# Relative-position bias written once and read back overlapping, and the order of the last matmul pair

## The chip, the cores and the metric

One core of one Trainium2 chip runs the whole kernel in one launch. The metric is the time of an execution on the device, in microseconds. Inputs and the output are float32 in device memory.

## The reference

The reference is a trunk of two layers over 256 tokens of 2048 features. Layer 0 is a differential attention with 8 heads, whose scores get a learned bias by relative position and a mask by chunks of 64 tokens, and a squared-ReLU MLP of width 8192. Then keys, values and forget gates are computed once, and layer 1 is a forgetting attention with 16 heads and a second MLP. RMS norms stand before each part and at the end. What the change touches is the bias of layer 0 (8 heads, 32 buckets):

```python
rel = key_pos[None, :] - q_pos[:, None]
bias = jnp.transpose(rel_table[t5_bucket(rel)], (2, 0, 1)).astype(f32)
mask = (key_pos[None, :] // CHUNK) <= (q_pos[:, None] // CHUNK)
s = jnp.where(mask, s + bias[None, :, None], NEG)
p = jax.nn.softmax(s, axis=-1)
```

and, in matmuls of every part, `h @ w_qkv`, `hn @ w_k`, `h @ w_q` and `h @ w_in`. The bias depends only on key position minus query position, so each head has one row of 383 values, of which a query sees 256 that shift by one from query to query.

## The kernel before, in words

Every product with a weight matrix is done in split precision. ScalarE rounds a raw weight tile to its high part (L180, tile whi), VectorE subtracts it from the raw tile to get the low part (L183, wlo), and the activations are kept as high and low parts side by side. TensorE adds the products of high with high, high with low and low with high.

The weights come in granules of 512 KB (128 x 1024 floats), 768 in all, loaded by SyncE's DMA queue (L172) into 4 raw buffers; high and low parts have 5 buffers each. A load goes out when the low part that used its raw buffer is done, so a granule is asked for about seven steps ahead of its use, and split about four steps ahead.

There are two kinds of units. Token-major units (mm_b, L194 to L196) are for values, output projections and the MLPs' second products: eight or more granules of 2 weight rows of 512 columns. Feature-major units (mm_a, L209 and L212) are for queries, keys and the MLPs' first products: four granules of 4 weight rows of 256 columns, each row in two halves of 128; each half takes one matmul of the high part with 512 columns (high and low activations) and one of the low part with 256 columns (high activations). In the last of the 16 rows (k == 15) the low part goes first, so that the matmul with the stop flag is the one that covers all 512 columns. After a unit, ScalarE copies the columns 256 to 511 of both halves (L315) and VectorE adds the columns 0 to 255 (L316).

The order of work is written out by hand. A list of steps has one granule each; at step s the lists pre[s], then the casts of later granules, mid[s], the low parts and loads, the matmuls of step s and post[s] are put out in this order, and each engine works through its own instructions in that order. A DMA takes its place in the instruction order of the engine that issues it, and the engine's later instructions wait behind a wait of it.

The bias is made at the start. At step 5 TensorE multiplies the table by a one-hot matrix (bias_rows, L338): 8 rows of 383 values. At step 6 VectorE copies them (L342), and SyncE writes them to F in device memory (L344), 128 times over for each head. At step 8 SyncE reads them back into T (L352): partition q gets, from copy q of each head, 256 values from an offset that moves back by one from copy to copy. POOL then masks 64 columns of the first 64 queries (L353). The softmax of each head uses T in VectorE's scaling of the scores (L415), first at about 86 us.

In step 6, ScalarE's squares for the first norm (L252) stand ahead of the bias in pre[6]; in step 8 the evacuation of the first value unit (L380) and the cast of the gate weights (L967) stand ahead of it in pre[8].

Of the kernel before, what the change touches and what calls it, by code (L numbers as in the profile page):

```python
# [11 lines left out]
F32 = mybir.dt.float32  # L12
# [8 lines left out]
P = 128  # L21
D = 2048
S = 256
HD = 128
FF = 8192
NA = 8
# [3 lines left out]
NEG = -1e30  # L30
# [4 lines left out]
NREL = 383  # L35
# [7 lines left out]
def kernel(ctx: ExitStack, tc: tile.TileContext, *args):  # L43
    (x, rel_table, attn_g, mlp_g, w_qkv, lq1, lk1, lq2, lk2, subln_g, w_o_a, kv_g,
     w_k, w_v, w_f, b_f, w_q, w_o_b, w_in, w_out, fin_g, onehot, out) = args
    nc = tc.nc
# [5 lines left out]
    dr = ctx.enter_context(tc.tile_pool(name="dr", bufs=1, space=DRAM))  # L52
# [29 lines left out]
    h = [sb.tile([P, 2, CW], F32, tag=f"h{c}", name=f"h{c}") for c in range(NCH)]  # L82
# [115 lines left out]
    def mm_a(u, g, k0):  # L198
        bank, xs = u.bank, u.xs()
        hi = g.hi.rearrange("p (k c) -> p k c", k=g.kk)  # L200
        lo = g.lo.rearrange("p (k c) -> p k c", k=g.kk)
        for j in range(g.kk):
            k = k0 + j
            xt = xs[k // 2][:, k % 2, :]
            for n in range(2):
                w = slice(n * P, (n + 1) * P)

                def whole():
                    nc.tensor.matmul(bank[n], hi[:, j, w], xt, start=k == 0, stop=k == 15)  # L209

                def part():
                    nc.tensor.matmul(bank[n][:, 0:S], lo[:, j, w], xt[:, 0:S], start=False, stop=False)  # L212

                if k == 15:
                    part()
                    whole()
                else:
                    whole()
                    part()


    def new_x(tag):
# [111 lines left out]
    bias = {}  # L334
# [5 lines left out]
    def bias_out():  # L340
        bs = sb.tile([NA, 512], F32, tag="e", bufs=2, name="bs")
        nc.vector.tensor_copy(out=bs[:, 0:NREL], in_=bias["p"][0:NA, 0:NREL])  # L342
        F = dr.tile([NA, P, NREL], F32, tag="F", name="F")
        nc.sync.dma_start(out=F, in_=bs[:, 0:NREL].unsqueeze(1).broadcast_to([NA, P, NREL]))  # L344
        bias["F"] = F

    def bias_in():
        T = sb.tile([P, NA, S], F32, tag="tnc", bufs=2, name="T")

        src = bias["F"].rearrange("h q r -> h (q r)")[:, 127:127 + P * (NREL - 1)]  # L350
        src = src.rearrange("h (q r) -> q h r", r=NREL - 1)[:, :, 0:S]
        nc.sync.dma_start(out=T, in_=src)  # L352
        nc.gpsimd.memset(T[0:64, :, 192:256], NEG)  # L353
        bias["T"] = T

    def build_lambda():
# [38 lines left out]
    def diff_head(hd):  # L395
# [13 lines left out]
        def softmax(qt):  # L409
            def run():  # L410
                nk = P * (qt + 1)
                sc = st["sc", qt]
                s = sb.tile([P, 2, S], F32, tag="ssb", bufs=2, name="ssb")
                b = bias["T"][:, hd, S - nk:S].unsqueeze(1).broadcast_to([P, 2, nk])
                nc.vector.scalar_tensor_tensor(out=s[:, :, 0:nk], in0=sc[:, :, 0:nk], scalar=SCALE, in1=b,  # L415
                                               op0=ALU.mult, op1=ALU.add)
                nm = sb.tile([P, 2], F32, tag="nm", bufs=2, name="nm")
                nc.vector.tensor_reduce(out=nm, in_=s[:, :, 0:nk], op=ALU.max, axis=AX.X, negate=True)
                e = sb.tile([P, 2, S], F32, tag="e", bufs=2, name="e")
                rs = sb.tile([P, 2], F32, tag="rsum", bufs=2, name="rsum")  # L420
                for c in range(2):
                    nc.scalar.activation(out=e[:, c, 0:nk], in_=s[:, c, 0:nk], func=AF.Exp,
                                         bias=nm[:, c:c + 1], accum_out=rs[:, c:c + 1])
                st["e", qt] = e, rs
            return run
# [497 lines left out]
    n, ng = len(order), len(grs)  # L923
# [27 lines left out]
    for k in range(2):  # L951
        w = slice(k * CW, (k + 1) * CW)
# [24 lines left out]
    n0.plan(7, lag=2)  # L977
    post[5].append(bias_rows)
    pre[6].append(bias_out)
    pre[8].append(bias_in)  # L980
    pre[12].append(build_lambda)

    ns = LA - 1
    for s in range(n + 2):
# [13 lines left out]
        if s < n:  # L998
            u, i, ms = order[s]
            if u.bank is None:  # L1000
                if u.apart:
                    u.bank = [ps.tile([P, 512], F32, tag="sc", name="sc") for _ in range(2)]
                else:
                    u.acc = ps.tile([P, 2, 512], F32, tag="acc", name="acc")
                    u.bank = [u.acc[:, m, :] for m in range(2)]
                if u.start is not None:
                    u.start(s)
            g = u.gs[i]
            if u.kind == "B":
                mm_b(u, g, 2 * i, ms)  # L1010
            else:
                mm_a(u, g, 4 * i)
            if i == len(u.gs) - 1:
                u.done(u, s, ms)
# [4 lines left out]

def bucket_onehot():  # L1020

    rel = np.arange(-255, NREL - 255)
    n = np.abs(rel)
    large = 8 + sum((n >= t).astype(np.int64) for t in (12, 16, 23, 32, 46, 64, 91))
    b = np.where(rel > 0, 16, 0) + np.where(n < 8, n, large)
    return (np.arange(32)[:, None] == b[None, :]).astype(np.float32)
# [25 lines left out]
```

## Time and profile before

| what | value |
|---|---|
| median of 3 runs | 2245.37 us (2244.74 to 2245.7) |
| the profiled execution's own time | 2244.49 us |
| its span, first to last instruction | 2242.7 us |
| mean granted TensorE clock | 0.994 |
| TensorE matmul busy | 2213.4 us |
| VectorE, ScalarE busy | 1356.7 us, 1020.8 us |
| moved by DMA | 416.06 MB, mean 186 GB/s |

An engine's busy time is the time in which its instructions run; starts are counted from the first instruction. Matmuls are pipelined, so that a row's duration is longer than the distance to the next start, and a stretch of TensorE is best read from the starts. The granted clock is a share of 2.4 GHz; 0.50 is 1.2 GHz. Issuing a DMA is not counted as busy time.

### The profile page before, as it was taken

What the parts mean: (1) busy time and instruction counts of PE and PEld (TensorE: products, weight loads), DVE (VectorE), ACT (ScalarE), POOL (GpSimd) and SP (SyncE); (2) the same over time, 40 slices, a digit from 0 to 9 for tenths busy, and PEclk for the clock granted to TensorE, in tenths of its full rate; (3) what the DMA queues carried; (4) which work ended last, traced back from release to release, by engine and by line L of the source; (5) the groups of instructions that cost most, each with busy time, mean ns of one, the idle gap of its engine ahead of it and who ended that gap; (6) DMA issues with size and microseconds to landing.
All of it is one profiled execution on the core that took longest, in us unless ns stands there. A gap on an engine that the chain in (4) does not pass through costs nothing.

```text
span 2242.7 us, 28986 instructions
## 1 busy us (share of the span) xinstructions
PE 2213.4 (99%) x11272; PEld 1877.7 (84%) x11272; DVE 1356.7 (60%) x1768; ACT 1020.8 (46%) x1343; POOL 13.6 (1%) x19
## 2 busy tenths in 40 slices
PE   8799999999999999999999999999999999999998
PEld 6688888888888888888888888888888888888886
DVE  4566666665565566566576566656655655655655
ACT  4455545544344344344554444454434444444443
POOL 0000000000000000000001000000000000000000
PEclk9899999999999999999999999999999999999999
DMA  7665555556656656655556565556566566566564
GB/s 199 199 183 172 166 170 183 173 188 201 183 185 202 195 180 195 192 187 189 177 170 204 173 194 186 180 170 201 183 200 189 185 193 186 188 197 180 187 202 135
DMA packets 319332, 416.06 MB, mean 186 GB/s; under 512 B 15066, under 2 KB 218972, under 8 KB 319068
## 3 DMA queue, kind: packets, MB, share of 16 engines
q1 hardware_dynamic: 319148, 414.20, 58.9%
q8 instruction: 88, 1.44, 0.3%
q14 instruction: 48, 0.39, 0.1%
q10 hardware_dynamic: 48, 0.02, 0.0%
HBM read 410.49 MB, written 3.68 MB: 185 GB/s over the span
## 4 chain that ended last, share of the span: by engine, by line
PE 97%; DMA 2%; DVE 0%; ACT 0%; issue 0%; SPq 0%; DVEq 0%; ACTq 0%
PE acc L209 32%; PE acc L212 16%; PE acc L194 15%; PE acc L196 15%; PE acc L195 15%; DMA raw<-in_w_qkv_a 2%; PE tp L232 1%; PE sc L405 0%; PE sc L748 0%; PE sc L194 0%; PE sc L195 0%; PE sc L196 0%; PE o L806 0%; DMA h<-in_x 0%; PE fp L619 0%; PE o L807 0%
## 5 line engine op out<-in xcount | busy, mean ns | idle before, releaser
L183 DVE TENSOR_TENSOR wlo<-raw,whi 128x1024 fp32r<-128x1024 f32 x767 | 926.1, 1225 | 627.4 <-ACT whi L180 626.8
L180 ACT CAST whi<-raw 128x1024 fp32r<-128x1024 f32 x767 | 795.9, 1048 | 730.5 <-PE acc L196 443.5
L209 PE MATMUL acc<-x,whi 128*128 128x512 f32 x2816 | 996.1, 399 | 17.5 <-ACT whi L180 17.5
L212 PE MATMUL acc<-x,wlo 128*128 128x256 f32 x2816 | 777.7, 281 | 0.5 <-DVE wlo L183 0.5
L209 PEld LDWEIGHTS acc<-x,whi 128*128 128x128 f32 x2816 | 525.7, 188 | 139.6 <-ACT whi L180 17.8
L212 PEld LDWEIGHTS acc<-x,wlo 128*128 128x128 f32 x2816 | 532.9, 189 | 9.2 <-DVE wlo L183 1.0
L194 PE MATMUL acc<-whi,hx 128*128 128x512 f32 x1120 | 436.9, 390 | 0.0
L196 PE MATMUL acc<-whi,hx 128*128 128x512 f32 x1120 | 436.0, 389 | 0.0
L195 PE MATMUL acc<-wlo,hx 128*128 128x512 f32 x1120 | 435.8, 389 | 0.0
L196 PEld LDWEIGHTS acc<-whi,hx 128*128 128x128 f32 x1120 | 210.2, 188 | 43.8
L195 PEld LDWEIGHTS acc<-wlo,hx 128*128 128x128 f32 x1120 | 210.3, 188 | 43.5
L194 PEld LDWEIGHTS acc<-whi,hx 128*128 128x128 f32 x1120 | 210.3, 188 | 43.1
L316 DVE TENSOR_TENSOR zs<-acc,z 128x512 f32<-128x512 f32 x96 | 66.3, 691 | 103.8 <-ACT z L315 103.8
L315 ACT COPY z<-acc 128x512 f32<-128x512 f32 x96 | 56.3, 587 | 157.9 <-PE acc L209 157.9
L590 ACT CAST hx<-s 128x512 fp32r<-128x512 f32 x64 | 39.7, 620 | 143.3 <-DVE s L588 143.3
L194 PE MATMUL acc<-whi,x 128*128 128x512 f32 x256 | 103.4, 404 | 0.0
L195 PE MATMUL acc<-wlo,x 128*128 128x512 f32 x256 | 100.5, 393 | 0.0
L196 PE MATMUL acc<-whi,x 128*128 128x512 f32 x256 | 100.5, 392 | 0.0
L209 PE MATMUL acc<-hx,whi 128*128 128x512 f32 x256 | 91.6, 398 | 0.0
L591 DVE TENSOR_TENSOR hx<-s,hx 128x512 fp32r<-128x512 f32 x64 | 44.3, 692 | 43.9 <-ACT hx L590 43.9
L212 PE MATMUL acc<-hx,wlo 128*128 128x256 f32 x256 | 70.5, 281 | 0.0
L327 DVE TENSOR_TENSOR h<-acc,h 128x512 f32<-128x512 f32 x88 | 56.7, 686 | 14.9 <-PE acc L196 14.9
(172 smaller groups left out, 1169.8 us busy)
## 6 DMA issues: line engine op xcount, KB each, us to landing
raw<-in_w_mlp_in SPq DMA_DIRECT2D x256, 512.0 KB, 4.0
raw<-in_w_mlp_out SPq DMA_DIRECT2D x256, 512.0 KB, 4.2
raw<-in_w_qkv_a SPq DMA_DIRECT2D x96, 512.0 KB, 4.5
raw<-in_w_o_a SPq DMA_DIRECT2D x32, 512.0 KB, 4.3
raw<-in_w_v_b SPq DMA_DIRECT2D x32, 512.0 KB, 3.8
raw<-in_w_k_b SPq DMA_DIRECT2D x32, 512.0 KB, 3.9
raw<-in_w_q_b SPq DMA_DIRECT2D x32, 512.0 KB, 4.2
raw<-in_w_o_b SPq DMA_DIRECT2D x32, 512.0 KB, 3.7
```

The source lines that it names most:

```text
L180: nc.scalar.copy(out=g.hi, in_=g.raw)
L183: nc.vector.tensor_tensor(out=g.lo, in0=g.raw, in1=g.hi, op=ALU.subtract)
L194: nc.tensor.matmul(bank[m], xh, hi[:, j, :], start=k == 0, stop=False)
L195: nc.tensor.matmul(bank[m], xh, lo[:, j, :], start=False, stop=False)
L196: nc.tensor.matmul(bank[m], xl, hi[:, j, :], start=False, stop=k == nk - 1)
L209: nc.tensor.matmul(bank[n], hi[:, j, w], xt, start=k == 0, stop=k == 15)
L212: nc.tensor.matmul(bank[n][:, 0:S], lo[:, j, w], xt[:, 0:S], start=False, stop=False)
L315: nc.scalar.copy(out=z1, in_=u.acc[:, :, S:2 * S])
L316: nc.vector.tensor_tensor(out=zs, in0=u.acc[:, :, 0:S], in1=z1, op=ALU.add)
L327: nc.vector.tensor_tensor(out=h[c][:, m, :], in0=u.bank[m], in1=h[c][:, m, :], op=ALU.add)
L590: nc.scalar.copy(out=t[:, :, 0:S], in_=s)
L591: nc.vector.tensor_tensor(out=t[:, :, S:2 * S], in0=s, in1=t[:, :, 0:S], op=ALU.subtract)
```

## The change: what it does

F now holds each head's 383 values once, in reversed order of position (the one-hot matrix is built with falling instead of rising positions). Both the write of F and the read of T are issued by ScalarE instead of SyncE, at the same places in the order. The read takes, for partition q and each head, the 256 values from offset q on, so that neighbouring partitions read overlapping pieces of the same row. T's columns are then in reversed order of keys; the mask is set on columns 0 to 63, and the softmax reads T backwards. In feature-major units all 16 rows put the high part first and the low part second, and the stop flag is on the low part's matmul.

```diff
@@ mm_a
             for n in range(2):
                 w = slice(n * P, (n + 1) * P)
-
-                def whole():
-                    nc.tensor.matmul(bank[n], hi[:, j, w], xt, start=k == 0, stop=k == 15)
-
-                def part():
-                    nc.tensor.matmul(bank[n][:, 0:S], lo[:, j, w], xt[:, 0:S], start=False, stop=False)
-
-                if k == 15:
-                    part()
-                    whole()
-                else:
-                    whole()
-                    part()
+                nc.tensor.matmul(bank[n], hi[:, j, w], xt, start=k == 0, stop=False)
+                nc.tensor.matmul(bank[n][:, 0:S], lo[:, j, w], xt[:, 0:S], start=False, stop=k == 15)
@@ bias_out, bias_in
-        F = dr.tile([NA, P, NREL], F32, tag="F", name="F")
-        nc.sync.dma_start(out=F, in_=bs[:, 0:NREL].unsqueeze(1).broadcast_to([NA, P, NREL]))
+        F = dr.tile([NA, NREL], F32, tag="F", name="F")
+        nc.scalar.dma_start(out=F, in_=bs[:, 0:NREL])
...
-        src = bias["F"].rearrange("h q r -> h (q r)")[:, 127:127 + P * (NREL - 1)]
-        src = src.rearrange("h (q r) -> q h r", r=NREL - 1)[:, :, 0:S]
-        nc.sync.dma_start(out=T, in_=src)
-        nc.gpsimd.memset(T[0:64, :, 192:256], NEG)
+        F = bias["F"]
+        src = bass.AP(F.tensor, F.offset, [[1, P], [NREL, NA], [1, S]])
+        nc.scalar.dma_start(out=T, in_=src)
+        nc.gpsimd.memset(T[0:64, :, 0:64], NEG)
@@ diff_head, softmax
-                b = bias["T"][:, hd, S - nk:S].unsqueeze(1).broadcast_to([P, 2, nk])
+                b = bias["T"][:, hd, 0:nk][:, ::-1].unsqueeze(1).broadcast_to([P, 2, nk])
@@ bucket_onehot
-    rel = np.arange(-255, NREL - 255)
+    rel = np.arange(127, 127 - NREL, -1)
```

## Rows read from the trace of the kernel before

**Rows 1.** The page, busy time (share of the span) and instructions of the engines.
```profile
PE 2213.4 (99%) x11272; PEld 1877.7 (84%) x11272; DVE 1356.7 (60%) x1768; ACT 1020.8 (46%) x1343; POOL 13.6 (1%) x19
```
**Rows 2.** Stretches: from:to, length, engines' busy time (instructions), granted clock, DMA share, GB/s.
```profile
40.00:60.00 20.00, 9.41 (x56) 8.00 (x54) 2.36 (x2) 1.01 (x2) 0.00 (x0) 0.79 0.56 77
60.00:80.00 20.00, 12.62 (x58) 10.53 (x59) 9.28 (x13) 7.79 (x10) 0.52 (x1) 0.70 0.74 224
...
300.00:1000.00 700.00, 700.00 (x3547) 594.26 (x3547) 421.49 (x494) 308.76 (x370) 0.00 (x0) 1.00 0.60 187
```
**Rows 3.** Waits of TensorE from 20 to 75 us: total, times, longest.
```profile
PE acc L209 <- ACT whi L180: 17.5, 1, 17.5
PE acc L212 <- DVE wlo L183: 0.5, 1, 0.5
```
**Rows 4.** Chain of waits, 20 to 75 us: start, us, what.
```profile
35.57 30.16 DMA raw<-in_w_qkv_a
```
**Rows 5.** Timeline of SyncE's queue: start, duration, DMA issued (several merged).
```profile
29.44 0.82 SPq L344 DMA_DIRECT2D F<-bs  x1
35.57 13.97 SPq L172 DMA_DIRECT2D raw<-in_w_qkv_a  x2
64.38 0.37 SPq L352 DMA_DIRECT2D T<-F  x1
64.85 5.13 SPq L172 DMA_DIRECT2D raw<-in_w_qkv_a  x4
```
**Rows 6.** Waits of SyncE's queue from 20 to 75 us.
```profile
SPq L352 <- DMA F<-bs: 14.8, 1, 14.8
```
**Rows 7.** Stretches of 4 us, columns as in rows 2.
```profile
32.00:36.00 4.00, 4.00 (x20) 3.07 (x19) 1.61 (x5) 3.20 (x6) 0.00 (x0) 1.00 1.00 329
...
56.00:60.00 4.00, 0.00 (x0) 0.00 (x0) 0.00 (x0) 0.00 (x0) 0.00 (x0) 0.50 0.46 49
...
68.00:72.00 4.00, 3.83 (x12) 3.35 (x13) 1.58 (x3) 0.92 (x2) 0.52 (x1) 0.50 1.09 378
```
**Rows 8.** Timeline of TensorE's matmuls; L209 is the high part, L212 the low.
```profile
49.13 0.28 PE L212 MATMUL acc<-x,wlo 128*128 128x256 f32 x1
66.91 0.80 PE L209 MATMUL acc<-x,whi 128*128 128x512 f32 x1 [17.50 <-ACT whi L180]
...
72.29 0.39 PE L209 MATMUL acc<-x,whi 128*128 128x512 f32 x1
...
77.23 0.40 PE L209 MATMUL acc<-x,whi 128*128 128x512 f32 x1
...
78.64 0.40 PE L209 MATMUL acc<-x,whi 128*128 128x512 f32 x1
```
**Rows 9.** Timeline of ScalarE: the casts of granules (two merged in a row).
```profile
33.25 1.98 ACT L180 CAST whi<-raw 128x1024 fp32r<-128x1024 f32 x2
...
39.01 2.00 ACT L180 CAST whi<-raw 128x1024 fp32r<-128x1024 f32 x2
...
71.37 1.05 ACT L180 CAST whi<-raw 128x1024 fp32r<-128x1024 f32 x1 [3.08 <-DMA raw<-in_w_qkv_a]
```
**Rows 10.** Timeline of VectorE: the bias copy and low parts.
```profile
28.87 0.55 DVE L342 COPY bs<-bp 8x383 f32<-8x383 f32 x1 [0.17 <-PE bp L338]
...
34.32 1.23 DVE L183 TENSOR_TENSOR wlo<-raw,whi 128x1024 fp32r<-128x1024 f32 x1 [4.91 <-ACT whi L180]
...
40.10 2.36 DVE L183 TENSOR_TENSOR wlo<-raw,whi 128x1024 fp32r<-128x1024 f32 x2 [0.25 <-ACT whi L180]
```
**Rows 11.** DMAs: one issue's duration; KB and us to landing; weight loads' landing, 24 to 75.
```profile
0.98 0.38 ACTq L94 DMA_DIRECT2D grow<-in_attn_norm_g  x1
...
grow<-in_attn_norm_g ACTq DMA_DIRECT2D x1, 16.0 KB, 2.7
...
C<-fg_nc SPq DMA_DIRECT2D x1, 16.0 KB, 4.7
...
NC<-C SPq DMA_DIRECT2D x4, 512.0 KB, 6.1
...
DMA to landing us min/median/max: 4.7/6.5/30.2
```
**Rows 12.** Who uses T: the mask on POOL, and the softmax's instructions (ns).
```profile
69.84 0.52 POOL L353 MEMSET T<- 64x512 f32 x1 [67.33 <-DMA T<-F]
...
L415 DVE SCALAR_TENSOR_TENSOR ssb<-sc,T x16: 415/554/685, 86.2 to 334.8; 128x256 f32<-128x256 f32 x8, 128x512 f32<-128x512 f32 x8
```

## The prediction

> **What bounds the kernel now.** I read the page's busy times first: TensorE works 99% of the span [rows 1], so only what stops or slows TensorE can matter. The stretch view says where the missing per cent lies: TensorE is busy 9.41 us of the 20 us from 40, at a granted clock of 0.79, and 12.62 us of the next 20 at 0.70, while the 700 us from 300 are full at 1.00 [rows 2]. The list of waits names the stop: one wait of 17.5 us of a high-part matmul for ScalarE's cast L180, and 0.5 us for the low part [rows 3]. The chain of waits goes one step further back: the cast waited for a weight load issued at 35.57 that took 30.16 us to land [rows 4].
>
> Why so long is read from SyncE's queue. At 29.44 it issued the write of F (8 x 128 x 383 x 4 bytes = 1.57 MB, out of 8 partitions). The two loads issued behind it, at 35.57 and after, held the queue 13.97 us in the issuing alone; then the read of T waited 14.8 us for F and went out at 64.38 [rows 5, 6]. In between the DMA engines were busy to 0.46 and moved 49 GB/s, against 329 GB/s before and 378 GB/s after [rows 7]. So F crawls on about half of the engines for 34.9 us (29.44 to 64.38), and the loads behind it in the same queue crawl with it. The stop is a DMA queue's, shown on TensorE.
>
> **What the stop costs.** Call a 512-column high matmul and its 256-column low one a pair. From 72.29 to 77.23 there are 14 pairs, 0.353 us each [rows 8]. The last low matmul before the stop starts at 49.13 and is followed a third of a pair later, so the next high one was due at 49.25; it starts at 66.91, and the engine is back at full speed only with the one at 72.29. Seven pairs run between 66.91 and 72.29, which cost 7 x 0.353 = 2.47 us at full clock. Lost: (66.91 - 49.25) + (5.38 - 2.47) = 17.66 + 2.91 = 20.57 us; the second term is the 0.5 us wait and the half clock (1.2 instead of 2.4 GHz) that the idle stretch left behind.
>
> **The change part by part.**
>
> F becomes 8 rows of 1532 bytes, 12 KB, and goes to ScalarE's queue. The bulk write is gone, and with it what the loads of granules 13 and 14 queued behind: -20.57 us if nothing else is late at that place. The steps are numbered as TensorE takes granules of 8 pairs, 2.82 us: granule 13 is the one due at 49.25, so 11 is due at 43.6, 14 at 52.1, 15 at 54.9, 16 at 57.7.
>
> ScalarE now issues two DMAs in its instruction order. F stands behind the eight squares of step 6, that is at 33.25 instead of 29.44; its source was copied by VectorE at 28.9 [rows 10], so it waits for nothing. The one DMA that this queue issued before cost 0.38 us, F's old issue on SyncE 0.82 [rows 5, 11]; I take 0.4. Behind it stand the casts of granules 9 and 10 (33.25 -> 33.65) and, through them, the low parts, the load of granule 13 (35.57 -> 36.0) and the norm chain. T's issue stands at step 8 behind the value evacuation and the cast of the gate weights; the casts of granules 11 and 12, at 39.01 before [rows 9], come behind it: 39.01 + 0.4 + 0.4 = 39.8. VectorE's low parts of 11 and 12 then end at 42.1 and 43.3 instead of 41.3 and 42.5 (1.23 each [rows 10]); 11 is due at 43.6, so 1.5 us are left, and both issues cost TensorE nothing. Without that cover they would cost 0.8 us.
>
> T's issue waits on ScalarE for F's landing. Transfers of 16 KB landed in 2.7 us at the start on ScalarE's queue and in 4.7 us later on SyncE's [rows 11], so F lands at 36.4 to 38.4, before ScalarE reaches T at 39.4: no wait. Bounds: 0, and 3.5 us under the first rival.
>
> One rule speaks against this. The Trainium skill (DMA: Bandwidth & Descriptors, "Queues, rings and completion order") states that a transfer's completion signal lands only after every earlier write of the same DMA engine, across its queues. By it F's landing would also wait for the four weight loads issued up to 29.1; no row here shows such a wait. Taken with the median of 6.5 us to landing of the loads of this stretch [rows 11] it would come at about 35.6, still ahead of 39.4, so by the rule the sum stays, and the first rival gets a part of its chance from it.
>
> T's megabyte now runs beside the weight loads in another queue. The nearest row: T and the two loads behind it, issued from 64.38 on, were in by 71.37, 7.0 us, at 378 GB/s [rows 5, 7, 9]. Used for granules 14 and 15, loaded at 39.6 and 42.1: in by 46.6 and 49.1, cast a microsecond later, due at 52.1 and 54.9. Granule 13, loaded at 36.0, lands by 43.0 even if it takes as long as that. Cover of 3 us or more everywhere: 0. The other end is F's own rate of 49 GB/s, which is the second rival. T itself is wanted by the softmax at 86.2 [rows 12], 20.57 earlier now, at 65.6; it is in by about 47 and its mask takes POOL 0.52 us.
>
> The mask on columns 0 to 63 and the one-hot table's order cost nothing. The reversed read of T on VectorE: 16 instructions of 0.415 to 0.685 us [rows 12], 8.8 us in all. No row shows a backward operand; between no change and twice the time I take no change. Even 8.8 us more would be spread over 250 us of an engine that is 60% busy, beside a TensorE that is not waiting for it: 0.
>
> The matmul order. 96 feature-major units (16 + 64 + 16) end today with low, high, low, high on their last row, which puts two short matmuls together and, at the next unit's start, two long ones. From the high matmul at 77.23 to the one at 78.64 lies such a place, 1.41 us for four pairs; four regular ones cost 4 x 0.353 = 1.41 [rows 8]. So the order is worth 0; by the rounding of the starts (0.02 us a place) between -1.9 and +1.9 us. The evacuation's first copy reads only columns that the last short matmul no longer writes, and may start 0.12 us sooner; TensorE does not wait for it.
>
> **Sum.** The profiled execution took 2244.49 us: 2244.49 - 20.57 = 2223.92. The median of the runs shown is 0.88 above it: 2224.8.
>
> **Rivals.**
>
> *ScalarE is held at T's issue*, by F's landing or because the issuing itself blocks, as SyncE's did behind F. If it is held until T is in (5.5 us, as from 64.38 to the mask at 69.84 [rows 5, 12]), granule 11 is cast at 44.9 to 46.0 and its low part ends at 47.2 against 43.7: 3.5 us, 2228.3. For it: the blocked issues of SyncE. Against it: those had F's 1024 pieces ahead of them, ScalarE's queue has 8; T's issue took 0.37 us once F was done.
>
> *T's read is the new crawl*: 128 partitions read overlapping pieces of the same 12 KB, beside the loads. At 49 GB/s T takes 21.4 us, to 61.2, and if granule 14 is held as long, TensorE stops from 52.1 to 62.2 and has 2.9 us of half clock: 13.1 us given back, 2237.9. It turns the change into a loss when T takes over 29.3 us (in at 68.7): 16.6 + 1.05 + 2.9 = 20.6 us of new stop. For it: no row shows this overlapping read. Against it: a broadcast read of 512 KB out of few rows landed in 6.1 us [rows 11], and the half-idle engines went with a transfer out of 8 partitions, T goes to 128.
>
> *The stop is not F's*: loads would be late there anyway, 2245.4. For it: what TensorE waited for was a weight load. Against it: loads landed within 1.5 us of F's end, and at 329 GB/s before F had the engines.
>
> **How the numbers follow.** Forecast 84% (2222.8 to 2226.8 by the order's bounds); ScalarE held 8%; T's crawl 3% short of a loss and 2% as a loss; not F's 3%. The range takes in the forecast's bounds and the first rival: 2222.8 to 2229. A measurement of this kernel can tell about 0.2%, 4.5 us, from no change: faster 0.95, no change 0.03, slower 0.02.
>
> **What would show it.** Right: no wait of L209 for L180 after 40 us; granted clock 1.00 from 40 to 80; F landing in under 5 us, T in under 10, both on ScalarE's queue; some 1.5 MB and 1000 packets less in all; softmax operations of unchanged length; the high matmul that stood at 72.29 at about 51.7. Wrong: a TensorE wait near 43.6 (ScalarE held) or near 52 (T), or a pair count in which a unit's end costs more than 1.41 us.

## The result, and the profile after

The changed kernel takes 2226.38 us (median of 4 runs, 2225.32 to 2227.27) against 2245.19 (4 runs); the ratio is 0.9916, with a 95% interval of 0.9899 to 0.9933. The forecast was 2224.8.

The page's busy times and its DMA total of the kernel after; the total was 416.06 MB in 319332 packets before.

```profile
span 2224.6 us, 28985 instructions
...
PE 2211.4 (99%) x11272; PEld 1875.3 (84%) x11272; DVE 1357.0 (61%) x1768; ACT 1020.6 (46%) x1343; POOL 13.3 (1%) x19
...
DMA packets 318317, 414.50 MB, mean 186 GB/s; under 512 B 15067, under 2 KB 217957, under 8 KB 318053
```

Stretches of the kernel after, columns as in [rows 2]:

```profile
40.00:60.00 20.00, 20.00 (x117) 17.43 (x116) 14.45 (x21) 10.62 (x14) 0.52 (x1) 1.00 0.87 261
60.00:80.00 20.00, 20.00 (x118) 17.47 (x117) 14.46 (x23) 9.74 (x17) 0.00 (x0) 1.00 0.64 203
```

TensorE is full and at its upper clock where it stood [rows 2]. From 20 to 75 us the list of its waits is empty; the waits of [rows 3] are gone.

ScalarE and its queue in the kernel after (timeline; ACTq is the issuing of a DMA):

```profile
33.77 0.63 ACT L241 ACTIVATE junk<-h 128x512 f32<-128x512 f32 x1
33.84 0.51 ACTq L333 DMA_DIRECT2D F<-bs  x1
34.31 0.19 ACT L241 ACTIVATION_READ_ACCUMULATOR junk<-h 128x1 f32 x1
34.40 1.99 ACT L180 CAST whi<-raw 128x1024 fp32r<-128x1024 f32 x2
38.71 0.69 ACT L369 ACTIVATE v<-acc,rstd 128x512 f32<-128x512 f32 x1 [2.32 <-DVE rstd L261]
39.12 0.40 ACTq L341 DMA_DIRECT2D T<-F  x1
39.30 0.68 ACT L369 ACTIVATE v<-acc,rstd 128x512 f32<-128x512 f32 x1
39.87 0.41 ACT L956 CAST wfs<-wf_raw 128x256 fp32r<-128x256 f32 x1
40.16 2.95 ACT L180 CAST whi<-raw 128x1024 fp32r<-128x1024 f32 x3
47.05 1.05 ACT L180 CAST whi<-raw 128x1024 fp32r<-128x1024 f32 x1 [3.93 <-DMA raw<-in_w_qkv_a]
```

Both DMAs are issued while ScalarE still computes what stands ahead of them: F at 33.84 beside the last square, T at 39.12 beside the value evacuation. The casts behind them stand 1.15 us later than in [rows 9], and this profile as a whole is 1.12 us late by then (below). T goes out without waiting for F. It landed 6.4 us after its issue and was masked at 45.59 (69.84 before); the softmax instructions that read it backwards keep their lengths, 415, 554 and 685 ns.

Where the time went is read best by pairing the matmuls of the two runs: 11272 in each, in the same order but for the last rows of units. Three starts serve as marks: the first feature-major matmul, the one at 72.29 in [rows 8], and the last one of all. Timeline of TensorE, first the kernel before, then after:

```profile
34.62 0.50 PE L209 MATMUL acc<-x,whi 128*128 128x512 f32 x1
...
2233.09 0.39 PE L196 MATMUL sc<-whi,hx 128*128 128x512 f32 x1
```

```profile
35.74 0.50 PE L207 MATMUL acc<-x,whi 128*128 128x512 f32 x1
...
50.43 0.40 PE L207 MATMUL acc<-x,whi 128*128 128x512 f32 x1
...
52.90 0.40 PE L207 MATMUL acc<-x,whi 128*128 128x512 f32 x1
...
2215.01 0.39 PE L196 MATMUL sc<-whi,hx 128*128 128x512 f32 x1
```

| | to the first mark | first to second | second to last |
|---|---|---|---|
| before | 34.62 | 37.67 | 2160.80 |
| after | 35.74 | 17.16 | 2162.11 |
| difference | +1.12 | -20.51 | +1.31 |

The matmul of 66.91 stands at 50.43, and the seven pairs behind it take 2.47 us. So the stop gave back 20.51 us; 1.12 were lost ahead of it and 1.31 behind it.

### The profile page after: what moved, and what is told of

Same layout as the page of the kernel before. It is cut to its first block, busy times and chain, and to the rows that moved or that the text cites. A ratio compares the mean times of both kernels' runs of the same rounds, so it can differ in the third digit from the quotient of the medians.

```text
span 2224.6 us, 28985 instructions
## 1 busy us (share of the span) xinstructions
PE 2211.4 (99%) x11272; PEld 1875.3 (84%) x11272; DVE 1357.0 (61%) x1768; ACT 1020.6 (46%) x1343; POOL 13.3 (1%) x19
## 4 chain that ended last, share of the span: by engine, by line
PE 99%; DMA 0%; DVE 0%; ACT 0%; SPq 0%; issue 0%; DVEq 0%; ACTq 0%
PE acc L207 32%; PE acc L208 16%; PE acc L194 15%; PE acc L196 15%; PE acc L195 15%; PE tp L221 1%; PE sc L737 0%; PE sc L394 0%; PE sc L196 0%; PE sc L194 0%; PE sc L195 0%; PE o L795 0%; DMA h<-in_x 0%; PE fp L608 0%; PE o L796 0%; PE tpo L472 0%
## 5 line engine op out<-in xcount | busy, mean ns | idle before, releaser
L207 PE MATMUL acc<-x,whi 128*128 128x512 f32 x2816 | 998.9, 399 | 0.0
L208 PE MATMUL acc<-x,wlo 128*128 128x256 f32 x2816 | 790.6, 281 | 0.0
L207 PEld LDWEIGHTS acc<-x,whi 128*128 128x128 f32 x2816 | 529.1, 188 | 130.0
L208 PEld LDWEIGHTS acc<-x,wlo 128*128 128x128 f32 x2816 | 532.0, 189 | 0.9
L207 PE MATMUL acc<-hx,whi 128*128 128x512 f32 x256 | 91.9, 401 | 0.0
L208 PE MATMUL acc<-hx,wlo 128*128 128x256 f32 x256 | 71.9, 281 | 0.0
L316 DVE TENSOR_TENSOR h<-acc,h 128x512 f32<-128x512 f32 x88 | 56.6, 685 | 14.9 <-PE acc L196 14.9
```

The lines of the kernel that those rows point to most:

```text
L316: nc.vector.tensor_tensor(out=h[c][:, m, :], in0=u.bank[m], in1=h[c][:, m, :], op=ALU.add)
```

## The experiments

The same three differences, read in the same way from each run's trace:

| run | what | median us | ratio to before (95%) | start | to second mark | rest |
|---|---|---|---|---|---|---|
| changed kernel | | 2226.38 | 0.9916 (0.9899 to 0.9933) | +1.12 | -20.51 | +1.31 |
| e9 | the same again | 2225.41 | 0.9912 (0.9897 to 0.9927) | 0.00 | -20.52 | +1.31 |
| e1 | bias part alone | 2223.82 | 0.9906 (0.9892 to 0.9919) | +0.01 | -20.62 | -0.11 |
| e2 | order part alone | 2246.44 | 1.0006 (0.9997 to 1.0014) | +0.02 | +0.35 | +1.73 |
| e3 | bias part, SyncE's queue | 2225.27 | 0.9913 (0.9899 to 0.9926) | -0.13 | -20.52 | +1.31 |

**e1, bias part alone, and e2, order part alone.** Edits: the `mm_a` hunk taken back, and the `mm_a` hunk alone.

> The bias part of the change alone (the matmul order of before). Theory: the whole gain is the removed write of F. Then the stop at granule 13 is gone and the time is that of before less 20.5 us, 2224.7, less what the order part costs in the changed kernel: aligned matmul by matmul, the changed kernel gains 20.5 us at the stop, loses 1.1 us ahead of it and 1.3 us spread over the rest. If the 1.3 us are the order's, this run is 1.3 us faster than the changed kernel (about 2225); if they are chance, the two agree. Rival (the order part carries some of the gain): slower than the changed kernel by more than 2 us.

> The order part alone (F written in bulk and read back as before). Theory: the stop stays, and the order costs 0.5 to 1.5 us: 2245.7 to 2246.7, with the pairs of some attention units at 353 ns instead of 347. Rival (order is worth something): below 2243.

Measured: 2223.82 and 2246.44. Without the order part the stop's 20.6 us come back and nothing is lost afterwards; with it the rest is longer by 1.3 us beside the bias part and 1.7 alone (0.5 of these right behind the second mark). So the gain is the bias part's alone, and the order part costs something. By the intervals of the ratios that cost cannot be told from none; it is the paired starts that show it.

**e9, the changed kernel again.**

> The changed kernel once more, unedited, beside the next two. Its first profile began 1.1 us later than the kernel before, at TensorE's wait for the first load of x; in five other profiles of kernels with the same start this difference was between -0.2 and +2.1 us. Theory (a chance of the first load's landing): another start here, within -0.3 and +2.2 us, the rest as before, -20.5 at the stop and +1.2 to +1.4 after it; 2224.5 to 2227.5. Rival (the change makes the start slower): again 1.1 us.

Measured: 2225.41; no late start, the other two differences as before. The 1.12 us at the start were a chance of that profile: TensorE waited 2.5 us for the first load of x there, 0.5 us in the kernel before, 0.7 in e9 and between 0.7 and 2.2 us in other runs.

**e3, both DMAs on SyncE.**

```diff
-        nc.scalar.dma_start(out=F, in_=bs[:, 0:NREL])
+        nc.sync.dma_start(out=F, in_=bs[:, 0:NREL])
...
-        nc.scalar.dma_start(out=T, in_=src)
+        nc.sync.dma_start(out=T, in_=src)
```

> F written once and T read overlapping as in the changed kernel, but both issued by SyncE instead of ScalarE. Theory (the bytes and pieces of F were the cost, not whose queue it was): no stop, within 1 us of the changed kernel, 2225 to 2227.5; F goes out 4 us earlier, T's read stands ahead of two loads in one queue. Rival (the move to another queue is what freed the loads): TensorE waits near 43 to 55 us, 2230 or more.

Measured: 2225.27, no TensorE wait. The move to ScalarE's queue is worth nothing: with F small, T's read went out of SyncE's queue at 39.56 without a wait and the loads behind it were in time.

**e4, F written late.** F's write moved from step 6 to step 8, right ahead of T's read.

```diff
-    pre[6].append(bias_out)
+    pre[8].append(bias_out)
     pre[8].append(bias_in)
```

> F's write issued by ScalarE at step 8, right ahead of T's read, instead of step 6, so that ScalarE stands at T's issue for F's whole landing. Theory (cover of 1.5 us for the low part and 2.7 us for the high part of granule 11, F lands 2.5 to 4 us after its issue): the casts of granules 11 and 12 come 2.5 to 4.5 us later and TensorE stops 1 to 3 us near 43.6: 2227.5 to 2229.5. Rival (more cover than counted, or ScalarE does not stand): same as the changed kernel, under 2227.

Measured: 2227.42 (0.9921, 0.9906 to 0.9936). Waits from 20 to 75 us of ScalarE, then of TensorE (whole run), then ScalarE's queue:

```profile
ACT whi L180 <- DMA F<-bs: 4.1, 1, 4.1
```

```profile
PE acc L208 <- DVE wlo L183: 0.8, 1, 0.8
PE acc L207 <- ACT whi L180: 0.5, 1, 0.5
```

```profile
41.13 0.51 ACTq L333 DMA_DIRECT2D F<-bs  x1
43.59 0.40 ACTq L341 DMA_DIRECT2D T<-F  x1
44.02 3.89 ACT L180 CAST whi<-raw 128x1024 fp32r<-128x1024 f32 x4 [4.10 <-DMA F<-bs]
```

T can go out 2.5 us after F's issue began. The casts waited 4.1 us, and TensorE lost 1.8 us at granule 11 (its stretch between the first two marks is 18.98 us against 17.16). That is the first rival's mechanism, at the place it named, made to happen by a later F; the cover at that place is about 2 us. The time is 0.1 us below the range that was expected.

**e5, e6, e7, e12: what made the old write expensive.** Each is the changed kernel plus a write of the old F's bytes that nobody reads, so that no instruction waits for it.

```diff
+        G8 = dr.tile([NA, P, NREL], F32, tag="G8", name="G8")
+        nc.sync.dma_start(out=G8, in_=h[0][0:NA, 0, 0:NREL].unsqueeze(1).broadcast_to([NA, P, NREL]))
```

That is e5, behind F's write at step 6 (the profile calls the new tile G). In e6 it is issued by `nc.scalar` behind T's read; in e7 its source is `h[0][:, 0, 0:NREL]`, 128 partitions with 8 copies each; in e12 a piece has 384 floats.

> The changed kernel, and beside it a write of the old F's size and shape (1.57 MB, 1024 pieces of 1532 bytes out of 8 partitions, from a tile of x, which nobody reads) issued by SyncE at step 6, where F's write stood. No instruction waits for it. Theory (loads queue behind such a write): the stop at granule 13 is back, 17 to 18 us plus some 3 us of half clock, 2243 to 2247. Rival (what cost the time was that T waited for F and held SyncE's queue): no such wait here, so no stop of that size, under 2232.

> The changed kernel with the same extra write issued by ScalarE right behind T's read, in ScalarE's queue, which carries nothing else later; again nobody waits for it. Theory A (only the order within one queue hurts; across queues the DMA engines take turns and a load passes the slow write): at most small stops, 2226 to 2231. Theory B (a slow piece holds its engine for about 0.27 us whoever comes next: 34.9 us for 128 pieces per engine): loads alternate with slow pieces on the 8 engines and land in 9 to 10 us or more, TensorE is starved for part of some 33 us: 2233 to 2245.

> The changed kernel with an extra write of the same 1.57 MB in the same 1024 pieces of 1532 bytes, but out of 128 partitions, issued by SyncE at step 6. Theory (8 source partitions, not the bytes, make the write slow): it runs on all 16 engines at 300 GB/s or more, 4 to 5 us, and the loads behind it are 4 to 5 us late, which the cover of some 4 to 6 us takes: no stop or under 2 us, 2226 to 2229. Rival (1.57 MB of writes is slow from anywhere): stop of over 10 us, 2237 or more.

> As the run with the extra write in SyncE's queue (1024 pieces of 1532 bytes out of 8 partitions, 2247 us, stop back), with pieces of 1536 bytes, 384 instead of 383 floats. Theory (few source partitions make the pieces slow): the stop is back all the same, 2244 to 2249. Rival (the odd length of 1532 bytes makes them slow; the packet records show 214 to 228 ns a piece of it out of 8 partitions against 84 ns for 2048-byte pieces of the loads): pieces at some 70 ns, the write done in about 10 us, stop under 3 us, 2226 to 2230.

| run | extra write | median us | ratio to before (95%) |
|---|---|---|---|
| e5 | 8 partitions, SyncE's queue | 2247.38 | 1.001 (1.0 to 1.0019) |
| e12 | the same, 1536-byte pieces | 2247.52 | 1.0011 (1.0001 to 1.002) |
| e6 | 8 partitions, ScalarE's queue | 2242.33 | 0.9987 (0.9978 to 0.9997) |
| e7 | 128 partitions, SyncE's queue | 2227.05 | 0.9919 (0.9903 to 0.9936) |

TensorE's waits from 20 us on in e5, in e6 and in e7 (L207 is the high part, L208 the low):

```profile
PE acc L207 <- ACT whi L180: 15.4, 2, 10.1
PE acc L208 <- DVE wlo L183: 0.9, 2, 0.5
```

```profile
PE acc L207 <- ACT whi L180: 8.8, 2, 6.1
PE acc L208 <- DVE wlo L183: 1.4, 3, 0.5
PE sc L396 <- DVE k L311: 1.1, 1, 1.1
```

```profile
PE acc L208 <- DVE wlo L183: 1.4, 2, 0.8
PE acc L207 <- ACT whi L180: 0.3, 1, 0.3
```

A write that nobody waits for brings the whole stop back (e5). TensorE waits twice there, and ScalarE's timeline tells for what:

```profile
33.43 0.51 ACTq L333 DMA_DIRECT2D F<-bs  x1
...
48.30 0.40 ACTq L343 DMA_DIRECT2D T<-F  x1
48.74 1.99 ACT L180 CAST whi<-raw 128x1024 fp32r<-128x1024 f32 x2 [8.88 <-DMA F<-bs]
68.05 1.04 ACT L180 CAST whi<-raw 128x1024 fp32r<-128x1024 f32 x1 [17.32 <-DMA raw<-in_w_qkv_a]
```

The longer wait, 10.1 us, stands at granule 13, as the stop of the kernel before does: its load, issued behind the extra write, was in only at 68.05. That alone sets when TensorE goes on, at 69.14. The first wait, 5.3 us at granule 11, is the first rival's: F's 12 KB, in ScalarE's queue and beside the write, let T go out 14.9 us after F's issue (2.5 in e4), and the casts behind T waited 8.9 us. It takes up part of a stop that the load would have made in any case. So T's wait on SyncE's queue is not needed for the stop; in the kernel before, too, the load that TensorE waited for was issued at 35.57, ahead of T's read in that queue [rows 5].

In ScalarE's queue the write costs 5 us less than in e5, but goes out 8.3 us later, at 38.22 behind T's read (e6). There the DMA view gives the loads' median landing in that stretch, 38 to 80 us:

```profile
raw<-in_w_qkv_a SPq DMA_DIRECT2D x10, 512.0 KB, 16.3
G<-h ACTq DMA_DIRECT2D x1, 1532.0 KB
T<-F ACTq DMA_DIRECT2D x1, 1024.0 KB, 7.2
```

16.3 us instead of the 5.3 that the changed kernel has from 28 to 66 us. Two loads land at 60.4 and 68.7, ahead of the write's last piece at 72.5: loads get past the slow write, and still starve. The Trainium skill (DMA: Bandwidth & Descriptors, "Queues, rings and completion order") states that an engine goes round the queues it has work for; these landings agree with it. The same bytes and pieces out of 128 partitions cost 2.3 us by the paired starts (e7); by the packet records they moved in 8.8 us, against 30.2 in e5. (That is half as fast as e7's expectation had it; the times of e6, by its theory B, of e7 and of e12 lie inside their ranges, that of e5 0.4 us above.) The trace's packet records give the piece: a median of 214 ns for a 1532-byte piece out of 8 partitions in e5, 228 in the kernel before, 74 out of 128 partitions in e7. Rounding the piece to 1536 bytes changes nothing (e12, 213 ns). Why a piece is three times slower there is open: the number of source partitions, the engines in use and the layout of the target went together.

**e8, e10, e11: the matmul order.** The order's cost led to three other orders of a feature-major row: high, low, low, high (e8); eight high then eight low of a granule (e10); high, high, low, low (e11).

```diff
-            for n in range(2):
-                w = slice(n * P, (n + 1) * P)
-                nc.tensor.matmul(bank[n], hi[:, j, w], xt, start=k == 0, stop=False)
-                nc.tensor.matmul(bank[n][:, 0:S], lo[:, j, w], xt[:, 0:S], start=False, stop=k == 15)
+            whole(0), whole(1), part(0, k == 15), part(1, k == 15)
```

That is e11, with `whole` and `part` as in the kernel before. In e8 rows after the first are `whole(0), part(0, k == 15), part(1), whole(1, k == 15)`.

> The changed kernel with feature-major rows in the order high, low, low, high (first row of a unit as in the changed kernel). Each pair of rows then has one place of two short and one of two long matmuls, as the last row of before had. From the starts of the kernel before, such places take 119 and 232 ns, the alternating ones 117 and 237: 351 against 354 ns a pair, that is 3 ns x 3072 pairs = 9 us faster than the changed kernel if each place keeps its price (2217). Rival (the price of a place depends on the run of matmuls around it, 347 or 353 ns a pair, and is not a sum over places): anywhere from 2226 + 5 to 2226 - 15; no change in pair length would be 2226.

> The changed kernel with each granule's eight high-part matmuls first and then its eight low-part ones. If what counts is the number of places where a long and a short matmul meet (two of two in the changed kernel, one of two in the mirrored order, which gained 12 us aligned, one of eight here), the gain is larger than the mirrored order's: at 227 ns for long after long, as token-major units show, and 113 to 120 for short after short, 340 to 347 ns a pair against 354: 20 to 40 us below the changed kernel, 2186 to 2206. Rival (the mirrored order gained by its own alternation, and short matmuls in a row cannot hide their weight loads of 188 ns): eight shorts in a row at more than 130 ns, 2216 or more.

> The changed kernel with each row as high, high, low, low. Two long and two short in a row, as in the mirrored order with the places shifted by one. Count of places: as mirrored, 2211 to 2216. Rival (position in the row matters): outside of that.

Measured: e8 2213.21 (0.9861, 0.9846 to 0.9876), e10 2213.76 (0.9859, 0.9843 to 0.9876), e11 2211.54 (0.9852, 0.9837 to 0.9867). e11 beats both kernels, the changed one measured beside it (e9) by 13.9 us. Timelines of TensorE near 1000 us, of the changed kernel, e11 and e10:

```profile
999.93 0.40 PE L207 MATMUL acc<-x,whi 128*128 128x512 f32 x1
...
1002.76 0.40 PE L207 MATMUL acc<-x,whi 128*128 128x512 f32 x1
```

```profile
999.76 0.62 PE L207 MATMUL acc<-x,whi 128*128 128x512 f32 x2
1000.23 0.40 PE L210 MATMUL acc<-x,wlo 128*128 128x256 f32 x2
...
1002.55 0.63 PE L207 MATMUL acc<-x,whi 128*128 128x512 f32 x2
```

```profile
999.75 2.00 PE L209 MATMUL acc<-x,whi 128*128 128x512 f32 x8
1001.59 1.11 PE L211 MATMUL acc<-x,wlo 128*128 128x256 f32 x8
1002.54 0.86 PE L209 MATMUL acc<-x,whi 128*128 128x512 f32 x3
```

Eight pairs take 2.83, 2.79 and 2.79 us, 354 against 349 ns a pair; 5 ns on 3072 pairs would be 15 us, and 13.9 were measured. e11 came out as expected and e8 4 us below the 2217 that a sum over places gave. The count of places where long meets short does not predict the time: e10 has the fewest and its expectation of 20 to 40 us failed; its long matmuls take 230 ns in a row (1.84 us for eight), not the 227 that I had taken over from token-major units.

## Why the prediction was right, and where it was off

**The stop.** Predicted 20.57 us from three starts, the pair length and the half clock; measured 20.5 in the changed kernel, in e9 and in e3, 20.6 in e1. Its reading as F's slow write, not T's wait for it, holds: in e5 nobody waits for the write and the load behind it is late again, e3 has SyncE's queue without the write and no stop. Only the length of the crawl was off: by the packet records F's pieces moved from 34.58 to 63.98, 29.4 us; the 34.9 counted the 5 us in which the loads issued ahead had the engines.

**The queue.** The prediction said that the loads "crawl with it" because they stand behind F in one queue. That is half of it: in e6 the loads stand in another queue than the slow write and land in 16.3 us, and in e5 F's 12 KB, in ScalarE's queue, let T go out after 14.9 us instead of 2.5. Here the slow write held up what other queues had issued, too.

**ScalarE's two issues.** Priced at 0.8 us of delay under a cover of 1.5; they cost the casts 0.03 us, since an issue goes out while the instruction ahead of it still runs. The conclusion (nothing) stands, the price was too high. F landed before T was due, as said; e4 shows 2.5 us, just under the range of 2.7 to 4.7, and what it costs when ScalarE does stand there, 1.8 us. In the changed kernel F's landing cost nothing. Where it was late in e5, its pieces themselves moved late, the last until 47.69, 0.6 us ahead of T's issue. In e7 the last piece was done at 37.49 and T's issue came at 40.28, 2.8 us later, when ScalarE had been free since 39.11; in e4 this distance is 0.5 us. The Trainium skill (DMA: Bandwidth & Descriptors, "Queues, rings and completion order") states that a completion signal lands only after every earlier write of the same engine; e7's delay agrees with it, but no run shows it to be the cause.

**T beside the loads.** Predicted in 7.0 us and no wait; 6.4 here, 7.1 in e1, no wait of TensorE. The row behind the 7.0 was read too kindly: by 71.37 T and one load were in, the second landed at 72.77, 8.4 us after T's issue; the cover took that, too. (In the rival of T's crawl, 10.1 and 2.9 make 13.0, not 13.1.) Reversed reads: no change, as said.

**The order.** This term was mis-sized: "the order is worth 0; by the rounding of the starts between -1.9 and +1.9 us". It measured +1.3 us in four runs with the small F. The price was taken from one place at a unit's end, where it is indeed 1.41 us for four pairs in both kernels. But there are 78 places where one feature-major unit follows another at once, and at 33 of them the changed kernel takes 1.42, the prediction's own sign of being wrong; the mean goes from 1.408 to 1.413, 0.4 us in all. The larger part of the loss lies inside units of the attention parts, 0.8 of the 1.4 us by which e9 is behind e1 after the second mark (see the last section).

**The sum.** The profiled execution was forecast at 2223.92 and took 2226.58; the late start of 1.12 us, which was chance, and the order's 1.31 are 2.43 of the 2.66 between them. The 0.88 us that the forecast of 2224.8 adds for the median did not come again: the changed kernel's median, 2226.38, is 0.20 below its profiled execution. That these 0.88 us stood in for part of the order's cost is luck. In e9, without the late start, the median is 2225.41.

## What to carry to other kernels

Do not price a transfer that replicates data out of few partitions by its bytes alone: here 1.57 MB out of 8 partitions moved for 29 us, with the DMA engines busy to about 0.46, where the same bytes out of 128 partitions took 8.8 us. Its bill came 20 us after its issue as a TensorE stop, in the name of ScalarE's cast. Here it was enough to write the data once and let the read do the replication. And when two runs execute the same matmuls, pair them by number and subtract the starts: it splits a change of 18 us into three terms, of which one is chance, to a few hundredths of a microsecond.

## What was not expected of the hardware

Alternating long and short matmuls run at one of two paces, and keep it. From the bias part alone (e1), first two starts of a unit in which nine pairs take 3.12 us, then nine pairs of the same unit in the changed kernel, where they take 3.18:

```profile
53.08 0.39 PE L209 MATMUL acc<-x,whi 128*128 128x512 f32 x1
...
56.20 0.39 PE L209 MATMUL acc<-x,whi 128*128 128x512 f32 x1
```

```profile
52.90 0.40 PE L207 MATMUL acc<-x,whi 128*128 128x512 f32 x1
...
56.08 0.40 PE L207 MATMUL acc<-x,whi 128*128 128x512 f32 x1
```

That is 347 against 353 ns a pair, at the same clock and with the same instructions. Four units of the first attention run without other matmuls in between; all four run at 347 in e1 and none in the changed kernel, so the order of a unit's last row bears on the pace of the units behind it. The MLP's units run at 353 to 354 in both. What sets the pace was not found. No order tried reached 347 throughout; from 349 in e11 that would be about 6 us more (2 ns on 3072 pairs), an estimate from these rows.
